# Part of a small triangular inverse moved from VectorE to GpSimd, in a two-layer hybrid decoder trunk

## Chip, core and metric

One core of a Trainium2 chip runs the whole kernel. The metric is device time in microseconds, the median of several runs.

## What is computed

A trunk of two layers over 528 positions (16 learned meta tokens and a sequence of 512) with a model width of 1024, all in float32. Each layer normalizes its input, projects it, and feeds four causal token mixers (RWKV-7, Mamba-2 SSD, retention, RG-LRU); the mixer outputs are projected, merged by gates and added to the stream, and a SwiGLU block follows. The change is in the RWKV-7 mixer, which the reference writes as a recurrence over positions:

```python
def step(s, inp):
    r_t, w_t, k_t, v_t, a_t, b_t = inp
    sa = jnp.einsum('bhvk,bhk->bhv', s, a_t)
    s = s * w_t[:, :, None, :] + sa[..., None] * b_t[:, :, None, :] + v_t[..., None] * k_t[:, :, None, :]
    return s, jnp.einsum('bhvk,bhk->bhv', s, r_t)
...
_, y = lax.scan(step, s0, xs)
```

with 16 heads of width 64. The kernel computes it in chunks of 64 positions. Within a chunk, the influence of each position on later ones is a strictly upper triangular matrix X, and the inverse of I - X is needed.

## The kernel before

Activations lie with 128 channels on the partitions and 528 positions in the free dimension. A dense product (`dense`, line 228) takes weight blocks of 128 x 128. `load_raw` fetches eight blocks in one load from SyncE, `blocks8` splits them into a high part (`whi`, ScalarE, line 217) and a low part (`wlo`, VectorE, line 218), and TensorE does three products for each block (line 240). `raw`, `whi` and `wlo` have three buffers each. Dense products fill most of TensorE's time in every stage.

The RWKV mixer goes through eight pairs of heads in each layer, so 16 times in all. For a pair, `rwkv_front` prepares the chunk operands, `rwkv_inverse` makes the triangular inverses, `rwkv_back` runs the nine chunks one after the other, and `rwkv_finish` normalizes. In `layer` (line 1103), the generator `others` gives the work of the other three mixers and of the gates, and `fill` puts a share of it behind each inverse and behind each back part. The order in which each engine runs its instructions is then fixed when the program is built, by priorities; each engine works through its own list in order.

`rwkv_inverse` does the following. TensorE makes the chunk matrices (line 867), VectorE masks them (lines 869 and 870). The 32 x 32 diagonal blocks are gathered through device memory: four stores into `xd` (line 905) and one load into `Xl` (line 909, tile `E`), so that each of 36 partitions (nine chunks times four blocks) holds a whole block. GpSimd sets `Nl` (tile `NS`) to the identity. Then 31 steps follow, a = 31 down to 1, of two VectorE instructions each: a multiplication (line 917, into `sm`) and an addition (line 919, into `NS`), on a rows by 32 - a columns. Each instruction needs the one before it. The result goes out to `nd` (line 920) and back in the layout of the chunks (lines 926 and 927). In `rwkv_back`, VectorE transposes blocks of it (line 941), and TensorE uses them first at line 951.

GpSimd otherwise clears pads and small blocks (lines 328, 709, 710, 771, 780, 885, 910, 911, 924 and others), copies (lines 784, 872, 963), and takes a share of the final scaling in `finish` (line 1237), where VectorE does the rest (line 1239).

Of the kernel before, what the change touches and what calls it, by code (L numbers as in the profile page):

```python
# [16 lines left out]
MUL, ADD, SUB, MIN, MAX = ALU.mult, ALU.add, ALU.subtract, ALU.min, ALU.max  # L17
# [4 lines left out]
T = 528  # L22
# [30 lines left out]
OTHERS = 8 * (2 * DENSE + 2.6) + DENSE + 4 * (6 * DENSE + 10.4) + 4 * (6 * DENSE + 14.3)  # L53
F1, F2, F3 = 48.0, 33.0, 170.0
UV = 2
GK = 2, 3, 3
NCST0, NCST1 = COFF["qdec"], COFF["hb"]

# [31 lines left out]
class _Em:  # L90
# [626 lines left out]
    def rwkv_common(self, l, S, p):  # L717
# [13 lines left out]
        def normed():  # L731
            self.X = [self.split(self.normed(j, S[j]), self.hp, "hh", "hl") for j in range(NT)]
            self.r = None
# [9 lines left out]
        for j in range(NT):  # L743
            if j == UV:
                normed()
# [105 lines left out]
    def rwkv_inverse(self, l, j, fr, p, q):  # L851
        nc = self.nc
        g2, AR, bk, P, v, bv = fr
        lo, hi = slice(0, 64), slice(64, 128)


        XK = self.t(q, [C64, 2, 64], "XK")
        MR = self.t(q, [C64, 2, 64], "MR")
        strict = self.c("tri")[:, :64].unsqueeze(1).unsqueeze(1)
        incl = self.c("tri")[:, 64:].unsqueeze(1).unsqueeze(1)  # L860
        blocks = [slice(b, b + 32) for b in range(0, 128, 32)]
        for c0 in range(0, C64, 2):
            n = min(2, C64 - c0)
            cs = slice(c0, c0 + n)
            ps = self.bank(self.psr).rearrange("p (c s x) -> p c s x", c=2, s=4)[:, :n]
            for c in range(c0, c0 + n):
                nc.tensor.matmul(ps[:, c - c0], bk[:, c].rearrange("p s x -> p (s x)"), AR[:, c],
                                 start=True, stop=True)
            nc.vector.tensor_tensor(out=XK[:, cs], in0=ps[:, :, 1:3], in1=strict.broadcast_to([128, n, 2, 64]), op=MUL)
            nc.vector.tensor_tensor(out=MR[:, cs], in0=ps[:, :, 0::3], in1=incl.broadcast_to([128, n, 2, 64]), op=MUL)  # L870
        for opp, h in ((hi, 0), (lo, 1)):
            nc.gpsimd.tensor_copy(AR[opp, :, 1 + h], XK[opp, :, h])


        BK = self.t(q, [C64, 2, 64], "BK")
        for c0 in range(0, C64, 4):
            n = min(4, C64 - c0)
            ps = self.bank(self.psr)[:, :n * 128]
            for c in range(c0, c0 + n):
                nc.tensor.transpose(ps[:, (c - c0) * 128:(c - c0 + 1) * 128], bk[:, c].rearrange("p s x -> p (s x)"),  # L880
                                    self.c("ident"))
            nc.scalar.activation(BK[:, c0:c0 + n].rearrange("p c h x -> p (c h x)"), ps, AF.Copy)

        SV = self.t(q, [C64, 2, 64], "SV")
        nc.gpsimd.memset(SV[lo, 0, 0], 0.0)
        nc.gpsimd.memset(SV[hi, 0, 1], 0.0)
        for c0 in range(0, C64, 8):
            n = min(8, C64 - c0)
            ps = self.bank(self.psr).rearrange("p (c x) -> p c x", c=8)
            for c in range(c0, c0 + n):  # L890
                for rows, opp in ((lo, hi), (hi, lo)):
                    nc.tensor.matmul(ps[opp, c - c0], v[rows, c * 64:c * 64 + 64], self.c("cent", rows)[:, rows],
                                     start=True, stop=True)
            nc.scalar.activation(SV[hi, c0:c0 + n, 0], ps[hi, :n], AF.Copy)
            nc.scalar.activation(SV[lo, c0:c0 + n, 1], ps[lo, :n], AF.Copy)


        i = self.ninv
        self.ninv += 1
        xd = self.tc.dram_tile([C64, 128, 32], F32, name=f"xd{i}")  # L900
        nd = self.tc.dram_tile([C64, 128, 32], F32, name=f"nd{i}")
        for h in range(2):
            for i in range(2):
                b = blocks[2 * h + i]
                nc.sync.dma_start(out=xd[:, b].rearrange("c r t -> r c t"), in_=XK[b, :, h, 32 * i:32 * i + 32])
        nl = 4 * C64
        Xl = self.t(q, 1056, "E", parts=nl)
        Nl = self.t(q, 2 * TP, "NS", parts=nl)
        nc.sync.dma_start(out=Xl[:, :1024], in_=xd.rearrange("c (g i) t -> (c g) (i t)", g=4))
        nc.gpsimd.memset(Nl[:, :1024], 0.0)  # L910
        nc.gpsimd.memset(Nl[:, :1024:33], 1.0)

        X3, N3 = (x[:, :1024].rearrange("p (i t) -> p i t", i=32) for x in (Xl, Nl))
        for a in range(31, 0, -1):
            w = 32 - a
            pr = self.t(q, 288, "sm", bufs=2, parts=nl)[:, :a * w].rearrange("p (i t) -> p i t", i=a)
            nc.vector.tensor_tensor(out=pr, in0=X3[:, :a, a:a + 1].broadcast_to([nl, a, w]),  # L917
                                    in1=N3[:, a:a + 1, a:].broadcast_to([nl, a, w]), op=MUL)
            nc.vector.tensor_tensor(out=N3[:, :a, a:], in0=N3[:, :a, a:], in1=pr, op=ADD)  # L919
        nc.sync.dma_start(out=nd.rearrange("c (g i) t -> (c g) (i t)", g=4), in_=Nl[:, :1024])  # L920
        N = self.t(q, 2 * TP, "NS").rearrange("p (c h x) -> p c h x", c=C64, h=2)
        for rows, h in ((lo, 0), (hi, 1)):
            b0, b1 = blocks[2 * h:2 * h + 2]
            nc.gpsimd.memset(N[rows, :, 1 - h], 0.0)
            nc.gpsimd.memset(N[b1, :, h, :32], 0.0)
            nc.sync.dma_start(out=N[b0, :, h, :32], in_=nd[:, b0].rearrange("c r t -> r c t"))
            nc.sync.dma_start(out=N[b1, :, h, 32:], in_=nd[:, b1].rearrange("c r t -> r c t"))
        return XK, MR, BK, SV, N

    def rwkv_back(self, l, j, fr, iv, p, q):  # L930
# [29 lines left out]

        UV = self.t(q, [C64, 2, 64], "XK")
        for rows, h in ((hi, 0), (lo, 1)):
            nc.gpsimd.tensor_copy(UV[rows, :, h], SV[rows, :, h])


        def flat(x):
            return x.rearrange("p h x -> p (h x)")

        for c in range(C64):
# [7 lines left out]
            with self.soon():  # L977
                for rows, h in heads:
                    nc.vector.tensor_copy(UV[rows, c, h], ps[rows, rows])
            if c == C64 - 1:  # L980
# [5 lines left out]
            ps = self.bank(self.psr)[:, :128]  # L986
            nc.tensor.matmul(ps, flat(BK[:, c]), flat(UV[:, c]), start=True, stop=True)
            with self.soon():
# [10 lines left out]
        for c0 in range(0, C64, 4):  # L999
            n = min(4, C64 - c0)  # L1000
            ps = self.bank(self.psr).rearrange("p (c h x) -> p c h x", c=4, h=2)
            for c in range(c0, c0 + n):
                o = ps[:, c - c0]
                fs = [lambda: nc.tensor.matmul(o, flat(UV[:, c]), MR[:, c], start=(c == 0), stop=True)]
                if c:
# [64 lines left out]
    def others(self, l, X, G, tg, tok, n, YB, YC, YD):  # L1070
# [3 lines left out]
        def gate(k):  # L1074
            for _ in range(k):
                b, m = next(gates, (None, None))
                if b is not None:
                    G[b][m] = self.gate(l, b, m, X, tg, tok, n)
                    yield DENSE

        def pool(name):
            self.st2.close()
            self.st2 = ExitStack()
            self.p2 = self.pool(name, 1, stack=self.st2)
# [3 lines left out]
        for j in range(8):  # L1088
            yield from self.lru(l, j, X, self.p2, YD)
            yield from gate(GK[0])  # L1090
        self.st2.close()
# [3 lines left out]
        for j in range(4):  # L1095
            yield from self.ret(l, j, X, self.p2, YC)
            yield from gate(GK[1])
        pool("ssm")
        for g in range(4):
            yield from self.ssm(l, g, X, self.p2, YB)  # L1100
            yield from gate(GK[2])

    def layer(self, l, S, sst, sd):
# [8 lines left out]
        with ExitStack() as st:  # L1112
# [9 lines left out]

            left, slots = OTHERS + DENSE * min(32, 8 * GK[0] + 4 * GK[1] + 4 * GK[2]), [w for _ in range(NT) for w in (F1, F2)]
            slots[-1] = F3
# [226 lines left out]
```

## Time and profile before

| | |
|---|---|
| median of 3 runs | 3492.44 us (3487.52 to 3496.19) |
| the profiled execution, its own time | 3490.24 us |
| its span, from the first to the last instruction | 3488.5 us |
| TensorE, VectorE, ScalarE, GpSimd busy | 96%, 69%, 44%, 5% of the span |

Engines are named PE (TensorE), PEld (its weight loads), DVE (VectorE), ACT (ScalarE), POOL (GpSimd) and SP (SyncE). Matmuls are pipelined, so PE's busy time overlaps itself; the distance between starts tells the pace. `Lnnn` is a line of the kernel, `out<-in` the tiles. A number in brackets behind an instruction is the engine's idle time before it, and who ended it. PEclk is the granted TensorE clock, 1.00 being 2.4 GHz and 0.50 being 1.2 GHz.

### The profile page before, as it was taken

The page shows a single profiled execution, that of the slowest core. Times are in us where ns is not written, and L with a number is a line of the kernel's source. Part 1 is how long each engine was busy: PE and PEld are TensorE (multiplying, and loading weights), DVE is VectorE, ACT ScalarE, POOL GpSimd, SP SyncE. Part 2 cuts the span into 40 slices and gives each one's busy share as a digit, 9 for nine tenths or more (in the row PEclk, how much of TensorE's full clock was granted, in tenths as well). Part 3 has the DMA queues.
Part 4 walks back from the last instruction along what each step waited for, and adds up shares of the span by engine and source line. Part 5 has one row for each costly group of instructions (what it writes and reads, how often), then busy time and mean ns, then how long its engine had stood idle before and what let it go on. Part 6 is the DMA issues. An engine that isn't in the chain of part 4 may idle for free. (4 is left out here: it accounts for less than half of the span.)

```text
span 3488.5 us, 61174 instructions
## 1 busy us (share of the span) xinstructions
PE 3363.5 (96%) x24584; PEld 3072.4 (88%) x24584; DVE 2396.4 (69%) x4644; ACT 1533.7 (44%) x2282; POOL 184.9 (5%) x493
## 2 busy tenths in 40 slices
PE   8999999999999999999999998999999989999998
PEld 7999899999988999999988887888888887788887
DVE  7877877788987555453348788678878885555543
ACT  6665544455444324222335654445454353332222
POOL 1000100100000000000000001010000000000001
PEclk9999999999999999999999998999999999999999
DMA  4333332233233643223333233223322245533332
GB/s 130 98 104 96 98 92 84 78 98 90 90 106 122 189 150 107 89 90 104 120 105 107 88 103 95 80 74 101 96 81 84 80 129 170 178 109 97 96 97 85
DMA packets 171739, 365.48 MB, mean 105 GB/s; under 512 B 54880, under 2 KB 63712, under 8 KB 171456
## 3 DMA queue, kind: packets, MB, share of 16 engines
q1 hardware_dynamic: 169936, 360.09, 33.6%
q8 instruction: 194, 3.18, 0.4%
q10 hardware_dynamic: 1152, 1.05, 0.1%
q14 instruction: 89, 0.73, 0.1%
q0 software_dynamic: 368, 0.44, 0.0%
HBM read 309.47 MB, written 47.71 MB: 102 GB/s over the span
## 5 line engine op out<-in xcount | busy, mean ns | idle before, releaser
L240 PE MATMUL d<-hh,whi 128*128 128x264 f32 (+1 forms) x4928 | 1181.6, 307 | 26.3 <-ACT whi L217 10.4
L240 PE MATMUL d<-hl,whi 128*128 128x264 f32 (+1 forms) x4928 | 1178.8, 306 | 1.2 <-DVE hl L259 1.1
L240 PE MATMUL d<-hh,wlo 128*128 128x264 f32 (+1 forms) x4928 | 1173.7, 305 | 0.0
L217 ACT ACTIVATE whi<-raw 128x1024 fp32r<-128x1024 f32 (+1 forms) x462 | 485.6, 1051 | 1158.7 <-PE d L240 920.0
L240 PEld LDWEIGHTS d<-hh,whi 128*128 128x128 f32 x4928 | 803.1, 190 | 64.2 <-ACT whi L217 10.4
L240 PEld LDWEIGHTS d<-hl,whi 128*128 128x128 f32 x4928 | 801.3, 190 | 34.6 <-DVE hl L259 2.4
L240 PEld LDWEIGHTS d<-hh,wlo 128*128 128x128 f32 x4928 | 800.5, 190 | 30.1 <-issue 1.2
L218 DVE TENSOR_TENSOR wlo<-raw,whi 128x1024 fp32r<-128x1024 f32 (+1 forms) x462 | 561.0, 1215 | 264.3 <-ACT whi L217 246.2
L240 PE MATMUL d<-yh,whi 128*128 128x264 f32 (+1 forms) x768 | 205.8, 324 | 2.4 <-ACT yh L258 2.4
L240 PE MATMUL d<-yl,whi 128*128 128x264 f32 (+1 forms) x768 | 207.4, 324 | 0.4 <-DVE yl L259 0.4
L240 PE MATMUL d<-yh,wlo 128*128 128x264 f32 (+1 forms) x768 | 206.4, 322 | 0.0
L917 DVE TENSOR_TENSOR sm<-E,NS 36x31 f32<-36x31 f32 (+15 forms) x496 | 164.0, 331 | 14.3 <-DMA E<-xd 4.7
L919 DVE TENSOR_TENSOR NS<-NS,sm 36x31 f32<-36x31 f32 (+15 forms) x496 | 164.2, 331 | 9.4
L240 PEld LDWEIGHTS d<-yh,whi 128*128 128x128 f32 x768 | 126.6, 188 | 16.6 <-ACT yh L258 5.4
L240 PEld LDWEIGHTS d<-yl,whi 128*128 128x128 f32 x768 | 127.8, 188 | 13.2 <-DVE yl L259 1.8
L240 PEld LDWEIGHTS d<-yh,wlo 128*128 128x128 f32 x768 | 127.5, 188 | 10.6
L240 PE MATMUL d<-fh,whi 128*128 128x264 f32 (+1 forms) x506 | 132.3, 318 | 0.0
L240 PE MATMUL d<-fl,whi 128*128 128x264 f32 (+1 forms) x506 | 132.0, 317 | 0.0
L240 PE MATMUL d<-fh,wlo 128*128 128x264 f32 (+1 forms) x506 | 131.6, 316 | 0.0
L1183 DVE TENSOR_TENSOR fg<-d,nr 128x528 f32<-128x528 f32 (+1 forms) x44 | 30.8, 700 | 126.0 <-PE d L240 122.4
L1066 DVE SCALAR_TENSOR_TENSOR gth<-gth,d 128x528 f32<-128x528 f32 (+1 forms) x48 | 33.4, 696 | 99.3 <-PE d L240 99.2
L1188 DVE TENSOR_TENSOR fth<-d,fth 128x528 f32<-128x528 f32 (+1 forms) x44 | 30.8, 700 | 92.6 <-PE d L240 92.5
(606 smaller groups left out, 4655.0 us busy)
## 6 DMA issues: line engine op xcount, KB each, us to landing
raw<-w SPq DMA_DIRECT2D x462, 512.0 KB
g<-gth SPq DMA_DIRECT2D x32, 264.0 KB
Bs<-acd SPq DMA_DIRECT2D x32, 264.0 KB
gth<-g SPq DMA_DIRECT2D x32, 264.0 KB
g<-gth SPq DMA_DIRECT2D x32, 256.0 KB
gth<-g SPq DMA_DIRECT2D x32, 256.0 KB
yd<-lt SPq DMA_DIRECT2D x16, 264.0 KB
ya<-wy SPq DMA_DIRECT2D x16, 264.0 KB
```

What stands on the lines that cost most here:

```text
L217: nc.scalar.activation(hi[:, :n], raw[:, :n], AF.Copy)
L218: nc.vector.tensor_tensor(out=lo[:, :n], in0=raw[:, :n], in1=hi[:, :n].bitcast(F32), op=SUB)
L240: nc.tensor.matmul(ps[:, h], w[:, k - k0], xv[:, h], start=(k == 0 and w is hi and xi == 0), stop=(k == nk - 1 and w is lo))
L917: nc.vector.tensor_tensor(out=pr, in0=X3[:, :a, a:a + 1].broadcast_to([nl, a, w]), in1=N3[:, a:a + 1, a:].broadcast_to([nl, a, w]), op=MUL)
L919: nc.vector.tensor_tensor(out=N3[:, :a, a:], in0=N3[:, :a, a:], in1=pr, op=ADD)
L1066: nc.vector.scalar_tensor_tensor(out=v2(th), in0=v2(th), scalar=1.0, in1=pz, op0=ADD, op1=MUL)
L1183: nc.vector.tensor_tensor(out=v2(g), in0=pg, in1=v2(r), op=MUL)
L1188: nc.vector.tensor_tensor(out=v2(th), in0=pu, in1=v2(th), op=MUL)
```

## The change

Column t of the inverse depends only on columns of the same index in rows below it, so the columns can be computed in two groups. The first 22 columns get a tile of their own, `Pl` (in the buffer `wy`), which GpSimd sets to the identity. GpSimd does 21 steps on it, a = 21 to 1, with the product in the buffer `wy2`, and copies the 22 x 22 result into `Nl` at the end. VectorE keeps columns 22 to 31 for all 31 steps. Both read the same loaded block `Xl`.

```diff
+PI = 22
...
+        Pl = self.t(p, T, "wy", parts=nl)[:, :PI * PI]
+        nc.gpsimd.memset(Pl, 0.0)
+        nc.gpsimd.memset(Pl[:, ::PI + 1], 1.0)
+        P3 = Pl.rearrange("p (i t) -> p i t", i=PI)
         for a in range(31, 0, -1):
-            w = 32 - a
+            t0 = max(a, PI)
+            w = 32 - t0
             pr = self.t(q, 288, "sm", bufs=2, parts=nl)[:, :a * w].rearrange("p (i t) -> p i t", i=a)
             nc.vector.tensor_tensor(out=pr, in0=X3[:, :a, a:a + 1].broadcast_to([nl, a, w]),
-                                    in1=N3[:, a:a + 1, a:].broadcast_to([nl, a, w]), op=MUL)
-            nc.vector.tensor_tensor(out=N3[:, :a, a:], in0=N3[:, :a, a:], in1=pr, op=ADD)
+                                    in1=N3[:, a:a + 1, t0:].broadcast_to([nl, a, w]), op=MUL)
+            nc.vector.tensor_tensor(out=N3[:, :a, t0:], in0=N3[:, :a, t0:], in1=pr, op=ADD)
+            if a < PI:
+                w = PI - a
+                pr = self.t(p, T, "wy2", parts=nl)[:, :a * w].rearrange("p (i t) -> p i t", i=a)
+                nc.gpsimd.tensor_tensor(out=pr, in0=X3[:, :a, a:a + 1].broadcast_to([nl, a, w]),
+                                        in1=P3[:, a:a + 1, a:].broadcast_to([nl, a, w]), op=MUL)
+                nc.gpsimd.tensor_tensor(out=P3[:, :a, a:], in0=P3[:, :a, a:], in1=pr, op=ADD)
+        nc.gpsimd.tensor_copy(N3[:, :PI, :PI], P3)
```

The lists of all engines come out in another order. GpSimd's list of the changed kernel, in the first inverse, holds the chain between the pad memset of a convolution (`xc`) and its next memsets. `wy` and its numbered forms are the tiles `Pl` and the product, `E` is the loaded block. Its line numbers are those of the changed kernel.

```order
L329 MEMSET xc 128x3 [waits DVE_49,PE_49,Pool_49]
L930 ISA
L930 TENSOR_TENSOR wy_786<-E,wy 36x21 [waits DMAHW0_49]
L932 TENSOR_TENSOR wy<-wy,wy_786 36x21 [waits Pool_49]
L930 TENSOR_TENSOR wy_792<-E,wy 36x40 [waits Pool_49]
L932 TENSOR_TENSOR wy<-wy,wy_792 36x20x2 [waits Pool_49]
```

The first multiplication waits for a DMA (the load of the block) alone, each later one for GpSimd's own instruction before it. The chain ends so:

```order
L932 TENSOR_TENSOR wy<-wy,wy_906 36x21
L933 COPY NS<-wy 36x22x22
L329 MEMSET xc 128x3
L781 MEMSET E 128x9
```

The next convolution's pad memset stands behind the chain and its copy.

VectorE's list around the end of the first inverse, before: the last addition (L919), then work on the next pair's `r` and its norms, then the transposes (L941).

```order
L778 SCALAR_TENSOR_TENSOR ech<-m_221,lam 128x576
L919 TENSOR_TENSOR NS<-NS,sm 36x31
L280 TENSOR_TENSOR r<-rtmp,v 128x528
L795 TENSOR_SCALAR rtmp<-s 128x264 x2
L218 TENSOR_TENSOR wlo<-raw,whi 128x1024
L713 SCALAR_TENSOR_TENSOR r<-d,par,r 128x528
L826 TENSOR_TENSOR AR<-r,E 64x9x64
L941 STREAM_TRANSPOSE sm<-NS 32x288
```

The same place in the changed kernel (L926 is the addition, L955 the transposes):

```order
L926 TENSOR_TENSOR NS<-NS,sm 36x10
L374 TENSOR_TENSOR th_1324<-th_1324,lt 128x528
L375 SCALAR_TENSOR_TENSOR lt<-la,th_1324 128x528
L376 TENSOR_TENSOR lt<-g_1314,lt 128x528
L219 TENSOR_TENSOR wlo<-raw,whi 128x1024
L714 SCALAR_TENSOR_TENSOR k<-d,par,k 128x528
L777 TENSOR_SCALAR lam<-lam 128x528
L779 SCALAR_TENSOR_TENSOR ech<-m_221,lam 128x576
L955 STREAM_TRANSPOSE sm<-NS 32x288 x2
```

The scan over `lam` (L778, now L779) stood ahead of the last addition and now stands behind it, and the work on `r` has gone behind the transposes: the inverse ends earlier in the list, measured by the other work around it.

## Rows read from the trace of the kernel before

**Rows 1.** The page: span, and busy time of each engine.

```profile
span 3488.5 us, 61174 instructions
...
PE 3363.5 (96%) x24584; PEld 3072.4 (88%) x24584; DVE 2396.4 (69%) x4644; ACT 1533.7 (44%) x2282; POOL 184.9 (5%) x493
```

**Rows 2.** Busy time by stage: per engine busy us and instructions, then granted clock, DMA share, GB/s.

```profile
60.00:1050.00 990.00, 964.27 (x8043) 910.53 (x8044) 797.25 (x1770) 512.69 (x808) 75.40 (x205) 0.99 0.31 95
...
1780.00:2860.00 1080.00, 1017.86 (x7589) 911.06 (x7590) 851.67 (x1861) 542.77 (x860) 80.00 (x219) 0.97 0.31 94
```

**Rows 3.** The same view of the 16 inverse windows: the first, the last, sum and mean.

```profile
78.70:119.70 41.00, 39.97 (x314) 39.05 (x312) 38.81 (x87) 31.69 (x42) 0.27 (x3) 1.00 0.36 106
...
2704.20:2750.40 46.20, 44.12 (x332) 41.27 (x331) 44.53 (x110) 14.96 (x21) 0.00 (x0) 1.00 0.36 110
sum 638.90, PE 623.20 PEld 592.04 DVE 591.97 ACT 371.77 POOL 12.68; mean PE 38.95 PEld 37.00 DVE 37.00 ACT 23.24 POOL 0.79
```

**Rows 4.** What PE waited for: us in total, times, longest.

```profile
PE s L951 <- DVE ends L556: 11.4, 1, 11.4
PE s L951 <- DVE sm L941: 11.0, 13, 2.6
```

**Rows 5.** Timeline of DVE and PE at the eleventh inverse, then the stretch after it.

```profile
2151.09 3.43 DVE L193 RECIPROCAL dtd<-dtd 16x528 f32<-16x528 f32 x1
...
2155.95 0.40 PE L240 MATMUL d<-hh,wlo 128*128 128x264 f32 x2
2167.77 0.31 PE L951 MATMUL s<-sm,XK 32*32 32x32 f32 x2 [11.42 <-DVE ends L556]
...
2167.50:2183.00 15.50, 12.37 (x120) 10.94 (x120) 10.04 (x27) 2.40 (x6) 2.39 (x4) 0.51 0.30 93
```

**Rows 6.** DVE groups by shape: busy us, mean ns, idle before.

```profile
L919 DVE TENSOR_TENSOR NS<-NS,sm 36x256 f32<-36x256 f32 x16 | 6.6, 411 | 0.2
...
L919 DVE TENSOR_TENSOR NS<-NS,sm 36x31 f32<-36x31 f32 x32 | 6.1, 191 | 0.4
```

**Rows 7.** DVE groups of lines 218 and 372.

```profile
L218 DVE TENSOR_TENSOR wlo<-raw,whi 128x1024 fp32r<-128x1024 f32 (+1 forms) x462 | 561.0, 1215 | 264.3 <-ACT whi L217 246.2 <-PE s L269 9.4 <-PE d L240 4.4
...
L372 DVE SCALAR_TENSOR_TENSOR th<-th,xc 128x528 f32<-128x528 f32 x16 | 11.2, 703 | 2.6 <-ACT th L354 2.4
```

**Rows 8.** Dense products on PE: start, us.

```profile
1200.15 0.41 PE L240 MATMUL d<-yh,whi 128*128 128x264 f32 x2
1200.39 0.40 PE L240 MATMUL d<-yl,whi 128*128 128x264 f32 x2
```

**Rows 9.** GpSimd lines 1237 and 784: ns min/median/max.

```profile
L1237 POOL TENSOR_TENSOR acc<-acc,fr x6: 724/909/966, 3474.1 to 3483.5; 128x256 f32<-128x256 f32 x6
...
L784 POOL COPY Pc<-E x16: 190/196/3197, 40.9 to 2616.7; 128x9 f32<-128x9 f32 x16
```

**Rows 10.** Two dependent GpSimd memsets: start, us.

```profile
2163.48 0.57 POOL L924 MEMSET NS<- 64x576 f32 x1 [1.02 <-DMA nd<-NS]
2164.11 0.33 POOL L925 MEMSET NS<- 32x288 f32 x1
```

**Rows 11.** Timeline at the end of the kernel, DVE and GpSimd.

```profile
3473.96 3.51 DVE L1239 SCALAR_TENSOR_TENSOR acc<-acc,par,fr 128x256 f32<-128x256 f32 x5
3477.91 0.42 DVE L1225 SCALAR_TENSOR_TENSOR acc<-d,acc 128x256 f32<-128x256 f32 x1 [0.43 <-PE d L250]
...
3474.08 2.72 POOL L1237 TENSOR_TENSOR acc<-acc,fr 128x256 f32<-128x256 f32 x3 [40.52 <-DVE fr L1233]
```

**Rows 12.** Timeline where GpSimd copies and DVE work meet.

```profile
1977.95 1.69 DVE L218 TENSOR_TENSOR wlo<-raw,whi 128x1024 fp32r<-128x1024 f32 x1
...
2159.27 3.20 POOL L784 COPY Pc<-E 128x9 f32<-128x9 f32 x1 [1.48 <-ACT E L782]
...
2161.00 0.74 DVE L821 TENSOR_TENSOR bk<-lam,ech 64x576 f32<-64x576 f32 x1
2161.67 0.74 DVE L822 TENSOR_TENSOR bk<-k,ech 64x576 f32<-64x576 f32 x1
```

## The prediction, made before the changed kernel ran

> **What bounds the kernel now.** I read the page's engine table first. TensorE (PE) is busy 96% of 3488.5 us, VectorE (DVE) 69%, GpSimd (POOL) 5% [rows 1]; less VectorE work alone therefore buys nothing. By stage, the first layer's mixers (60 to 1050 us) and the second's (1780 to 2860 us) leave PE 25.7 and 62.1 us idle [rows 2]. The inverses lie in these stages. So I next cut out the 16 stretches from the first L917 to the last L919 of each inverse, the "windows": 41.0 us the first, 46.2 us the last, 638.9 us in all. In them PE is busy 623.2 us and DVE 592.0 us, 37.0 of 39.9 us per window [rows 3]. Both engines are full there. DVE works in order, so the 62 small instructions of an inverse stand in one file with the weight splits (wlo, L218) that PE lives on. GpSimd is busy 0.8 us per window.
>
> What a late inverse costs can be seen too. PE also works in order, and L951, its first use of the inverse, stands among dense products. It waits there 22.4 us in 14 waits, one of 11.4 us, the others 2.6 us at most [rows 4]: the order puts L951 almost exactly where the inverse becomes ready, with no slack behind it. The one long wait is the price list. DVE lost 3.43 us to a reciprocal between two inverse instructions and more to its neighbours; PE finished its products at 2156.4 us and started L951 at 2167.8, doing nothing between. After it TensorE's granted clock was 0.51 for 15.5 us, the 1.2 GHz level of its two [rows 5], so some 7.6 us more went.
>
> **Part 1, what DVE loses.** The triangular sweep multiplies and adds a*(32-a) elements for a = 31 to 1, 5456 per operation kind. The corner of 22 columns is the sum of a*(22-a), 1771. The 62 instructions stay (a = 22 to 31 whole, the other 21 steps 10 columns wide); only elements go. A 36x256 addition takes 411 ns, a 36x31 one 191 [rows 6]: 0.98 ns per element. 2 x 1771 x 0.98 ns = 3.5 us per inverse. The order also takes other work out of the windows: 434 other DVE rows become 367, of which the wlo splits fall from 85 to 71. 14 x 1.22 us and 53 x 0.70 us [rows 7] over 16 make 3.4 us. So a window holds 6.9 us less DVE work.
>
> **Part 2, what PE loses in cover.** Counted in the order, the dense products between the last L867 and the first L951 of each inverse fall from 5321 to 4647 over the 16. Two take 0.24 us [rows 8]; 674 of them are 81 us, 5.1 us per inverse. PE arrives that much sooner. If nothing disturbed DVE, it would be ready 1.8 us before PE (6.9 - 5.1).
>
> **Part 3, what GpSimd adds.** 42 TENSOR_TENSORs in a chain, each waiting for the one before, 3542 elements, and a copy of 484. Before, L1237 is the only such instruction: 128x256, 724 ns at the fastest. The smallest copy, 128x9, takes 190 ns at the fastest [rows 9]. That gives about 0.19 us + 2.1 ns per element. Dependent GpSimd instructions stand 0.06 us apart (0.57 us long, 0.63 from start to start [rows 10]). Alone, the chain takes 42 x 0.25 + 3542 x 0.0021 = 17.9 us, the copy some 0.6 us. That fits in the 34.8 us (39.9 - 5.1) that a window would have; alone it would end before DVE's part. The two memsets of the new tile run earlier, while the block is still being loaded; GpSimd is idle there, so I cost them nothing (without that cover 0.6 us at most, as the larger memset of rows 10). The one ISA row ahead of the first multiplication stands before its wait too, in the first inverse only: nothing.
>
> **Part 4, the shared port.** The two parts do not run beside each other freely. At the end of the kernel, GpSimd's L1237 and DVE's L1239, each reading two SBUF tensors, meet: five DVE instructions take 3.51 us, where one alone of that size (L1225) takes 0.42 [rows 11]. Three GpSimd instructions thus cost DVE at least (3.51 - 2.10)/3 = 0.47 us each. Undisturbed DVE instructions overlap by 0.07 us (L821 and L822 start 0.67 us apart and take 0.74 [rows 12]), which makes it (3.51 - 1.82)/3 = 0.56; I take 0.52, 2.0 ns per element. In the mixers a wlo split took 1.69 us instead of 1.22 beside a GpSimd copy, and a 9-element copy 3.20 us instead of 0.19 behind DVE work [rows 7, 9, 12]. Each blocks the other. The inverse's DVE instructions have two SBUF inputs too. So the chain delays DVE: at least 0, if it fits into DVE's own pauses; at most its whole duration alone without the pauses, 42 x 0.19 + 7.4 + 0.6 = 16 us. By the finish's rate it is 3542 x 2.0 ns = 7.1 us, and I add 1 us of the fixed shares: **8 us**, since rows 11 show this pair of operations itself.
>
> **The sum.** Per inverse DVE is late by 8 - 1.8 = 6.2 us, and PE, in order and without slack, stands still as long. Slow clock after it: 7.6 us followed an 11.4 us wait; in proportion 4 us (bounds 0 and 7.6). 16 x 10.2 = 163 us. The 81 us of dense products taken out of the windows may fill PE's idle time elsewhere in the mixers, 25.7 + 62.1 - 15.7 = 72 us; most of it is short waits for results, so 12 us (bounds 0 and 72). 163 - 12 = +151. The profiled execution took 3490.24 us, 2.2 below the median of 3492.44; 3490 + 151 = 3641, and I say **3642 us** for the median. With 4 us of delay per inverse (stall 2.2, clock 1.5) it is 3537; with 12 (10.2 and 7) 3753.
>
> What queues behind: on GpSimd, the pad memsets of the next convolution and of E stand behind the chain; on SyncE, weight loads stand behind the store of the inverse. Both delays are the same microseconds, not others. The corner's tiles wy and wy2 belong to the back part's result, free before an inverse starts and wanted only after it: nothing.
>
> **Rivals.**
> - DVE waits for whole GpSimd instructions: the upper end above, 16 us of delay. Stall 16 - 1.8 = 14.2 us, clock 7.6: 16 x 21.8 - 12 = +337, 3827 us. For it: DVE's 1.69 us split beside a copy; against: at the finish a pair of instructions takes less than the 0.72 and 0.42 us of its two durations together [rows 9, 11]. The Trainium skill (SBUF — State Buffer, "Who interferes with whom") states it as a rule: the port pair that the two engines share is an exclusive lock, kept for the whole instruction, and a VectorE instruction with two SBUF inputs meets it when GpSimd reads. The trace agrees that they exclude each other; that the lock spans the whole duration it does not bear out.
> - GpSimd ends last. If each of its 42 instructions waits behind two DVE instructions rather than one (a window has 37.0 us for about 90, 0.41 us each), the chain takes 17.9 + 42 x 0.82 = 52 us, with the copy 18 us more than the 34.8. With 7.6 us of slow clock: 16 x 25.6 - 12 = +398, 3888 us. It decides from about one DVE instruction of wait each (35 us). For it: the 3.20 us copy; against: dependent DVE instructions leave a pause in which GpSimd gets in.
> - Faster: GpSimd's reads fall wholly into pauses (delay under 1.8 us per inverse). The waits at L951 (22.4 us) and the slow clock after the long one (7.6) go, and 12 us of filler: 3450 us. For it: 2.9 us of DVE idle per window; against: 7.1 us of reads, and rows 11.
> - No difference: a delay of 2 to 3 us, repaid by the filler; 3490 us.
> - That the change does not do what it says: the order shows the chain on GpSimd waiting for the load of the block alone, so the two sweeps may overlap. I give it nothing.
>
> **How the numbers follow.** Forecast 0.54, whole instructions 0.12, GpSimd last 0.16, faster 0.10, no difference 0.08. A measurement of this kernel tells 0.3%, about 10 us, from no change. Slower 0.82, the same 0.08, faster 0.10. The range leaves out the two cases that are not slower, 0.18: it runs from a little under 3537 to where GpSimd ends last, 3520 to 3890.
>
> **What would show it.** Right: the windows stay near 40 us though they hold less work; DVE's 36-partition steps lengthen by a few tenths where GpSimd overlaps; GpSimd's steps start 0.5 us or more apart; PE waits at the first use of the inverse some 6 us, 16 times, with 1.2 GHz stretches after. Wrong: windows of 33 to 35 us and no new waits of PE there (the ports do not matter), or the last GpSimd step well after DVE's (the second rival).

## The result and the profile after

| | before | changed |
|---|---|---|
| median of 4 runs, us | 3491.34 | 3520.53 |
| lowest to highest, us | 3487.52 to 3496.19 | 3518.92 to 3527.08 |
| profiled execution, us | 3490.24 | 3527.08 |
| its span, us | 3488.5 | 3525.3 |

The ratio is 1.0092, 95% interval 1.0078 to 1.0106: 29 us slower, where +151 was forecast. The sign was right, the size five times too large, and 3520.5 is the very lower end of the range.

The page of the changed kernel: span, then busy time of each engine (against [rows 1]).

```profile
span 3525.3 us, 61924 instructions
...
PE 3378.0 (96%) x24584; PEld 3082.0 (87%) x24584; DVE 2398.5 (68%) x4644; ACT 1535.6 (44%) x2282; POOL 558.5 (16%) x1213
```

Mean granted clock of TensorE, before:

```profile
core 0: 3488.5 us, clock 0.987
```

and of the changed kernel:

```profile
core 0: 3525.3 us, clock 0.983
```

Read PE first, since it is the busiest. The span grew by 36.8 us, some 7 more than the medians, as the profiled execution of the changed kernel is the slowest of its four. PE's work is the same 24584 matmuls, but its busy time grew by 14.5 us, and span less busy time from 125.0 to 147.3, by 22.3. Together they are the 36.8. The 14.5 us agree with the clock: (1 - 0.983) x 3525.3 - (1 - 0.987) x 3488.5 = 14.6, which can be 3.5 us off, as the clocks are rounded.

Then DVE. It was to lose 3.5 us per inverse, 56 us in all, yet its busy time is 2 us *higher* than before. The page's groups of instructions show where most of it came back:

```profile
L924 DVE TENSOR_TENSOR sm<-E,NS 36x60 f32<-36x60 f32 (+29 forms) x496 | 160.7, 324 | 16.2 <-DMA E<-xd 5.4
L926 DVE TENSOR_TENSOR NS<-NS,sm 36x60 f32<-36x60 f32 (+29 forms) x496 | 159.6, 322 | 10.8
...
L930 POOL TENSOR_TENSOR wy<-E,wy 36x21 f32<-36x21 f32 (+6 forms) x336 | 171.7, 511 | 89.7 <-DMA E<-xd 60.3
L932 POOL TENSOR_TENSOR wy<-wy,wy 36x21 f32<-36x21 f32 (+6 forms) x336 | 180.4, 537 | 26.1
```

DVE's multiplications and additions take 320.3 us, 20.0 per inverse; by their sizes (a line through the steps of before that ran undisturbed) they would take 16.9. On GpSimd one instruction takes 511 to 537 ns here.

The windows of the 16 inverses, first and last L924/L926, as in [rows 3] (stretch and length, then busy us and instructions of PE, PEld, DVE, ACT, POOL, then clock, DMA share, GB/s):

```profile
78.90:115.10 36.20, 32.28 (x240) 31.39 (x239) 34.05 (x81) 23.98 (x30) 22.16 (x45) 0.91 0.28 85
...
2725.60:2781.10 55.50, 50.52 (x377) 47.22 (x377) 48.35 (x120) 21.51 (x30) 23.81 (x43) 0.97 0.30 92
sum 579.10, PE 536.16 PEld 500.08 DVE 534.61 ACT 306.88 POOL 349.27; mean PE 33.51 PEld 31.25 DVE 33.41 ACT 19.18 POOL 21.83
```

A window has 36.2 us, 3.7 less than before, not the 40 of the forecast. What PE waited for, in us, times, longest:

```profile
PE s L270 <- issue: 18.1, 5, 4.1
PE s L965 <- DVE sm L955: 11.4, 9, 2.2
PE d L241 <- DVE x L334: 6.4, 3, 3.9
...
PE d L241 <- DVE NS L926: 5.5, 1, 5.5
```

L965 is the old L951, the first use of the inverse. PE waits there *less* than before, 11.4 us against 22.4 [rows 4], and in no wait longer than 2.2. The new waits are elsewhere: at dense products and at L270, the matmuls of a convolution, for DVE work that stands behind the sweep in DVE's file or in the middle of it. L270 is the old L269, where the kernel before had

```profile
PE s L269 <- issue: 2.3, 4, 0.7
```

("issue": the profile names nothing that the engine waited for). The timelines name it. In the first inverse, for example, the timeline (start, duration, engine, line) has on PE:

```profile
102.30 2.10 PE L270 MATMUL s<-xc,gw 128*128 128x264 f32 x4 [3.92 <-issue]
```

and on DVE the tile it wanted, xc, and the sweep's last step:

```profile
101.45 0.75 DVE L334 SCALAR_TENSOR_TENSOR xc<-d,par,xc 128x528 f32<-128x528 f32 x1
...
114.90 0.16 DVE L926 TENSOR_TENSOR NS<-NS,sm 36x10 f32<-36x10 f32 x1
```

xc ends at 102.2, and the matmul starts 0.1 us later. GpSimd's copy of the corner, the end of its chain, comes well before DVE's last step:

```profile
103.52 0.59 POOL L933 COPY NS<-wy 36x484 f32<-36x484 f32 x1
```

In all 16 inverses this copy ends ahead of DVE's last step, by 6.3 us at the least. So GpSimd does not end last; what it does is make DVE's steps longer.

### The profile page after: what moved, and what is told of

It reads as the page before. It is cut to its first block, busy times and chain, and to the rows that moved or that the text cites. A ratio compares the mean times of both kernels' runs of the same rounds, so it can differ in the third digit from the quotient of the medians.

```text
span 3525.3 us, 61924 instructions
## 1 busy us (share of the span) xinstructions
PE 3378.0 (96%) x24584; PEld 3082.0 (87%) x24584; DVE 2398.5 (68%) x4644; ACT 1535.6 (44%) x2282; POOL 558.5 (16%) x1213
## 5 line engine op out<-in xcount | busy, mean ns | idle before, releaser
L930 POOL TENSOR_TENSOR wy<-E,wy 36x21 f32<-36x21 f32 (+6 forms) x336 | 171.7, 511 | 89.7 <-DMA E<-xd 60.3
L932 POOL TENSOR_TENSOR wy<-wy,wy 36x21 f32<-36x21 f32 (+6 forms) x336 | 180.4, 537 | 26.1
L924 DVE TENSOR_TENSOR sm<-E,NS 36x60 f32<-36x60 f32 (+29 forms) x496 | 160.7, 324 | 16.2 <-DMA E<-xd 5.4
L926 DVE TENSOR_TENSOR NS<-NS,sm 36x60 f32<-36x60 f32 (+29 forms) x496 | 159.6, 322 | 10.8
```

Source lines behind the costliest of these rows:

```text
L926: nc.vector.tensor_tensor(out=N3[:, :a, t0:], in0=N3[:, :a, t0:], in1=pr, op=ADD)
L930: nc.gpsimd.tensor_tensor(out=pr, in0=X3[:, :a, a:a + 1].broadcast_to([nl, a, w]), in1=P3[:, a:a + 1, a:].broadcast_to([nl, a, w]), op=MUL)
L932: nc.gpsimd.tensor_tensor(out=P3[:, :a, a:], in0=P3[:, :a, a:], in1=pr, op=ADD)
```

## The experiments

The theory after the result: the shared port of Part 4 costs DVE 3.1 us per inverse, 49.6 of the 58 us that it should have lost and did not, and the kernel pays for it about one to one. Rivals: the order of instructions, which the change also rearranged, costs the time; GpSimd's mere length does; its pads, late behind the chain, do. Each kernel edits the changed one unless said otherwise, and each ratio is against the kernel before on the same chip.

### The same order, less reading by GpSimd: e1, e2, e3

In these three the orders of PE, DVE and SP are row for row those of the changed kernel (ACT's differs in one row's place in e1 and e2; GpSimd's own list differs). e1 leaves the corner out and puts two memsets per step, somewhat shorter, in the place of GpSimd's two instructions, so that GpSimd's chain writes and, apart from one copy of the block and one of the result, does not read:

```diff
-                nc.gpsimd.tensor_tensor(out=pr, in0=X3[:, :a, a:a + 1]...
-                nc.gpsimd.tensor_tensor(out=P3[:, :a, a:], ...
+                if a == PI - 1:
+                    nc.gpsimd.tensor_copy(pr[:, :a], Xl[:, :a])
+                m = min(100 + int(2.5 * a * w), 484)
+                nc.gpsimd.memset(pr[:, :m], 0.0)
+                nc.gpsimd.memset(Pl[:, :m], 0.0)
```

> Left out: GpSimd's products and sums of the corner. In their place stand one copy that waits for the block and then memsets, two per step, of about the same length (roughly 0.3 to 0.5 us each), which write SBUF and read nothing. The lists of TensorE, VectorE and SyncE are the same, row for row, as in the changed kernel. Theory 'port': the changed kernel is slower because GpSimd's reads hold up VectorE's instructions with two SBUF inputs (their time per inverse is 20.0 us, where their sizes alone would give 16.9); without the reads the 62 steps fall to about 17 us per inverse and the time falls by about 30 us, to 3490 or below. Theory 'queue': the pad memsets behind the chain make it slow; the time stays near 3520. Theory 'order': the new lists make it slow; the time stays near 3520 although the steps fall to 17 us.

Measured: 3471.43 us, ratio 0.9953 (0.9941 to 0.9965). Groups of instructions in e1:

```profile
L924 DVE TENSOR_TENSOR sm<-E,NS 36x60 f32<-36x60 f32 (+29 forms) x496 | 135.8, 274 | 15.5 <-DMA E<-xd 4.7
L926 DVE TENSOR_TENSOR NS<-NS,sm 36x60 f32<-36x60 f32 (+29 forms) x496 | 134.9, 272 | 10.8
...
L934 POOL MEMSET wy<- 36x152 f32 (+6 forms) x336 | 119.6, 356 | 18.7
L933 POOL MEMSET wy<- 36x152 f32 (+6 forms) x336 | 118.1, 352 | 19.0
```

The steps take 270.7 us, 16.9 per inverse: as by size. DVE's busy time over the whole kernel is 2348.6 us, 49.9 below the changed kernel's, of which these two lines give 49.6. So all that GpSimd's reads cost DVE lies in these two lines: 3.1 us per inverse, 74 ns for each of 672 GpSimd instructions. Windows of e1, same view as above:

```profile
sum 530.10, PE 523.61 PEld 492.53 DVE 483.65 ACT 307.52 POOL 112.22; mean PE 32.73 PEld 30.78 DVE 30.23 ACT 19.22 POOL 7.01
```

33.1 us each, 3.1 less. GpSimd is busy 7.0 us per window here against 21.8: half of the memsets do not wait for the block, and many run ahead of the sweep. 287 of the 672 lie inside it, beside 240 of DVE's 992 steps, and those 240 take on average some 3 ns more than the others, by size. In the first, the convolution's wait of 3.92 us is one of 0.20:

```profile
101.08 1.13 PE L270 MATMUL s<-xc,gw 128*128 128x264 f32 x4 [0.20 <-issue]
```

e2 has the same edit with `m = min(8, 484)`, short memsets.

> As the run with the memset chain, but each memset covers 8 columns (about 0.1 us), so the chain takes some 5 to 8 us instead of 18 to 25; same lists again. Port: the same time as with the longer memset chain, within 4 us. Queue: clearly faster than it, by most of the 30 us. Order: both stay near 3520.

Measured: 3469.77 us, 0.9952 (0.9938 to 0.9966), steps 16.9. The length of the memsets makes no difference. But in both kernels GpSimd's chain also ends sooner than in the changed one (in the first inverse of e1 at 90.3 us, not 103.5), so a late end of the chain is tested by e3 and e4 and not here.

e3 keeps GpSimd's instructions but lets them do half the rows:

```diff
-                nc.gpsimd.tensor_tensor(out=pr, in0=X3[:, :a, a:a + 1]...
+                nc.gpsimd.tensor_tensor(out=pr[:, :(a + 1) // 2], in0=X3[:, :(a + 1) // 2, a:a + 1]...
...
-                nc.gpsimd.tensor_tensor(out=P3[:, :a, a:], ...
+                nc.gpsimd.tensor_tensor(out=P3[:, :(a + 1) // 2, a:], ...
```

> Left out: about half of the corner's rows in each GpSimd step; the 42 products and sums work on half of the elements, the lists of TensorE, VectorE, ScalarE and SyncE are those of the changed kernel. Port: VectorE's 62 steps take about 18.5 us per inverse, halfway between 16.9 and 20.0, and the time lies about halfway between the changed kernel and the memset chain, 3500 to 3510. Order or queue: 3515 to 3520.

Measured: 3484.65 us, 0.9993 (0.9985 to 1.0001), a miss below the 3500 to 3510 expected; the steps:

```profile
L924 DVE TENSOR_TENSOR sm<-E,NS 36x60 f32<-36x60 f32 (+29 forms) x496 | 143.0, 288 | 16.1 <-DMA E<-xd 5.3
L926 DVE TENSOR_TENSOR NS<-NS,sm 36x60 f32<-36x60 f32 (+29 forms) x496 | 142.9, 288 | 10.8
```

They take 17.9 per inverse: half the reads cost a third of the delay, not half. The timelines say why. In the changed kernel, at the same steps of the first inverse, GpSimd:

```profile
83.61 0.39 POOL L930 TENSOR_TENSOR wy<-E,wy 36x105 f32<-36x105 f32 x1
84.07 0.40 POOL L932 TENSOR_TENSOR wy<-wy,wy 36x105 f32<-36x105 f32 x1
84.55 0.40 POOL L930 TENSOR_TENSOR wy<-E,wy 36x112 f32<-36x112 f32 x1
85.03 0.41 POOL L932 TENSOR_TENSOR wy<-wy,wy 36x112 f32<-36x112 f32 x1
```

and DVE beside it:

```profile
84.22 0.46 DVE L924 TENSOR_TENSOR sm<-E,NS 36x192 f32<-36x192 f32 x1
84.72 0.45 DVE L926 TENSOR_TENSOR NS<-NS,sm 36x192 f32<-36x192 f32 x1
85.19 0.47 DVE L924 TENSOR_TENSOR sm<-E,NS 36x207 f32<-36x207 f32 x1
```

Before, without GpSimd, the same two steps on DVE:

```profile
82.92 0.35 DVE L917 TENSOR_TENSOR sm<-E,NS 36x192 f32<-36x192 f32 x1
83.31 0.35 DVE L919 TENSOR_TENSOR NS<-NS,sm 36x192 f32<-36x192 f32 x1
```

In e3, DVE:

```profile
84.05 0.35 DVE L924 TENSOR_TENSOR sm<-E,NS 36x192 f32<-36x192 f32 x1
84.44 0.35 DVE L926 TENSOR_TENSOR NS<-NS,sm 36x192 f32<-36x192 f32 x1
```

and GpSimd:

```profile
84.27 0.29 POOL L930 TENSOR_TENSOR wy<-E,wy 36x56 f32<-36x56 f32 x1
...
84.64 0.31 POOL L932 TENSOR_TENSOR wy<-wy,wy 36x56 f32<-36x56 f32 x1
```

Alone, DVE's steps start 0.39 us apart. Beside GpSimd steps 0.48 apart, DVE's stand 0.47 to 0.50 apart. Beside GpSimd steps 0.37 apart, they keep their 0.39. And 0.46 to 0.49 is GpSimd's own pitch at this size, as the last inverse of the changed kernel shows in a stretch with no DVE instruction beside it:

```profile
2742.11 0.38 POOL L930 TENSOR_TENSOR wy<-E,wy 36x112 f32<-36x112 f32 x1
2742.57 0.42 POOL L932 TENSOR_TENSOR wy<-wy,wy 36x112 f32<-36x112 f32 x1
2743.06 0.37 POOL L930 TENSOR_TENSOR wy<-E,wy 36x105 f32<-36x105 f32 x1
```

The two chains go **in lockstep**, at the pitch of the slower. My reading of it, argued and not shown, is that each reads while the other stands between two of its dependent instructions. Only what GpSimd's pitch exceeds DVE's own is lost, not the whole of its reads. It holds beyond this pair: over the 320 DVE steps of the changed kernel that are followed directly by the next and have a GpSimd step beside them, the mean pitch is 428 ns, and the mean of the longer of the two own pitches (each a line by size through undisturbed steps) is 431; in e3, over 298 steps, it is 361 against 365.

Time follows the steps: 16.9, 17.9, 20.0 us per inverse give 3471, 3485, 3520.5. From the first to the last, 16 x 3.1 = 49.6 us of steps make 49.1 us of time (48.5 by the two ratios). In this one order GpSimd's reads are thus the cause of nearly all of it, with at most some 6 us left for the pads (e4); the rest of the change, without them, gains 17 us. It also settles Part 1's size: a window of e1 holds 30.2 us of DVE work against 37.0 before [rows 3], 6.8 less.

### The pads behind the chain: e4

In the changed kernel DVE waited 5.4 + 1.1 us for L329, the pads of the next convolution, which stand behind the chain on GpSimd (tile and line that waited, us, times):

```profile
  DVE x L334: 5.4, 2
  DVE Bs L334: 1.1, 1
```

```diff
-        nc.gpsimd.memset(xc[:, T:T + 3], 0.0)
+        nc.vector.memset(xc[:, T:T + 3], 0.0)
```

> The pad memsets of the convolutions (48 of them, 0.1 us each on GpSimd) go to VectorE; all else as in the changed kernel, so no convolution waits behind the GpSimd chain. The lists change in some places. Queue: the time falls by 15 us or more. Port or order: within 8 us of the changed kernel, since only 6.5 us of VectorE's waits in the changed kernel are for these memsets.

Measured: 3515.45 us, 1.0083 (1.0070 to 1.0095), steps 20.1. The 5 us fit the 6.5 of the trace, but the intervals overlap: at most a small part.

### Smaller corners: e5, e6

```diff
-PI = 22
+PI = 16
```

> The corner is 16 columns instead of 22: 30 GpSimd instructions of at most 64 elements. All lists change. Theory 'lockstep': two chains of dependent instructions pass the port to and fro, so a VectorE step is stretched only to GpSimd's own pitch (0.25 us + 2.1 ns per element, 0.28 to 0.385 us here) where that is longer than its own (0.24 to 0.45 us). Summed over the 30 overlapped steps that is about 0.6 us per inverse: the 62 steps take 19.7 us, where their sizes alone give 19.1. Theory 'sum of holds' (2.0 ns for each GpSimd element is added to VectorE, as at the end of the kernel): 1360 elements x 2.0 ns = 2.7 us, 21.8 us. The time by lockstep is 3475 to 3490, no slower than before; by the sum 3500 or more.

Measured: 3481.64 us, 0.9980 (0.9970 to 0.9990); steps 19.9, where size alone makes 19.1, the expected lockstep 19.7 and the sum of GpSimd's reads 21.8 (1360 elements x 2.0 ns more). With `PI = 18`:

> The corner is 18 columns: 34 GpSimd instructions of at most 81 elements (pitch up to 0.42 us). Lockstep: the 62 steps take about 1.2 us more than the 18.5 us of their sizes alone, 19.7; time 3480 to 3495. Sum of holds: 1938 elements x 2.0 ns = 3.9 us more, 22.4 us; time 3505 or more.

Measured: 3499.16 us, 1.0032 (1.0020 to 1.0045); steps 19.9 (alone 18.5, lockstep 19.7, sum of reads 22.4). The steps speak for lockstep both times. The time of e6 lies above what its steps explain, and e5 and e6 have the same 19.9 yet stand 17.5 us apart. Their orders differ from each other and from the changed kernel's; that is the only other difference I know of, and e11 returns to it.

### One operand out of SBUF: e7

If the port is the cause, a DVE step that reads only one tensor from SBUF should not be stretched. The product goes to PSUM, so that the addition reads one operand from each; the multiplication still reads two from SBUF:

```diff
-            pr = self.t(q, 288, "sm", bufs=2, parts=nl)[:, :a * w].rearrange("p (i t) -> p i t", i=a)
+            pr = self.bank(self.psr)[:nl, :a * w].rearrange("p (i t) -> p i t", i=a)
```

> As the changed kernel with 22 columns, but VectorE's product goes to a PSUM bank instead of SBUF, so its additions have one SBUF input only. Port: the additions are no longer stretched; the wait stays with the products. The sum of the 62 steps' excess falls from 3.1 us to about half or less (apart from what PSUM itself adds, the same for each addition), GpSimd's chain gets shorter than 25.4 us, and the time lies under 3510. If the inputs do not matter (a plain rivalry of the two engines for SBUF): the additions stay as long as the products, time near 3520.

Measured: 3480.02 us, 0.9975 (0.9967 to 0.9984). Groups in e7:

```profile
L924 DVE TENSOR_TENSOR s<-E,NS 36x60 f32<-36x60 f32 (+29 forms) x496 | 163.8, 330 | 18.5 <-DMA E<-xd 7.6 <-ACT SV L896 0.6
L926 DVE TENSOR_TENSOR NS<-NS,s 36x60 f32<-36x60 f32 (+29 forms) x496 | 132.7, 268 | 10.7 <-DVE s L924 0.2
```

The addition takes 268 ns, as undisturbed in e1 (272); the multiplication still 330. Half of the delay is gone. That is shown by the steps; the time has an order of its own in it. A miss: GpSimd's chain did not get shorter, 25.3 us from its first to its last step against 25.4.

### The chain without the relief: e8

DVE does all 32 columns again (`t0 = a`), GpSimd computes its corner as well, and the copy of the result, which nobody uses, is left out.

> VectorE does all 32 columns as in the kernel before; GpSimd does its 42 instructions too, and its result is not used. This shows the price of the chain alone. Lockstep: the 62 steps take about 3 us more than 20.5, some 23.5 us per inverse, and the time is 40 to 55 us over the kernel before. Sum of holds: 27 us per inverse and 100 us or more. Only the lists matter: 20.5 us and no difference in the steps.

Measured: 3518.02 us, 1.0089 (1.0075 to 1.0103):

```profile
L924 DVE TENSOR_TENSOR sm<-E,NS 36x31 f32<-36x31 f32 (+15 forms) x496 | 188.1, 379 | 11.1 <-DMA E<-xd 1.1
L926 DVE TENSOR_TENSOR NS<-NS,sm 36x31 f32<-36x31 f32 (+15 forms) x496 | 185.5, 374 | 9.6
```

23.3 us per inverse against 20.5 by size: 2.8 us of delay, near the 3.1 of the changed kernel and far from the 27 us per inverse of the sum of holds. The time grew by 30 us, less than the 45 of the delay: a miss in the time. Its order is its own too.

### Both together: e9, e10

The product in PSUM, with PI = 16:

> Both remedies together: a corner of 16 columns, and VectorE's product in PSUM. Lockstep and port: the steps' excess over their sizes falls from 0.8 us (corner of 16 alone) to about 0.5 us per inverse, some 19.6 us; if the 0.8 us were the whole remaining price, the time is 3470 to 3482. If the gain of either came from its lists and not from the port, the two do not add and the time lies anywhere between 3475 and 3500.

Measured: 3480.88 us, 0.9984 (0.9976 to 0.9993), steps 19.7. Against e5 that is 0.2 us less in the steps and no difference in time. With PI = 18:

> A corner of 18 columns with the product in PSUM. Port: the excess falls from 1.4 us (corner of 18 alone) to about 0.8 us, the steps to 19.3 us per inverse, and the time falls below the 3499 of the corner of 18 by 10 us or more. Lists: it may fall or rise by up to 15 us whatever the steps do.

Measured: 3468.71 us, **0.9945** (0.9931 to 0.9959), steps 19.3:

```profile
L924 DVE TENSOR_TENSOR s<-E,NS 36x112 f32<-36x112 f32 (+29 forms) x496 | 163.4, 329 | 17.6 <-DMA E<-xd 8.0
L926 DVE TENSOR_TENSOR NS<-NS,s 36x112 f32<-36x112 f32 (+29 forms) x496 | 145.8, 294 | 10.1
```

It beats both kernels. The excess over the size, 0.8 us, is as expected; that steps of 19.3 us give a shorter time than the 19.7 of e9, 12 us, is more than 16 x 0.4.

### What an order alone does: e11, e12

e11 is the kernel *before* with e7's edit, no GpSimd part at all. It takes no work from DVE and adds none.

> The kernel before, without any GpSimd chain, with VectorE's product in PSUM. Port: nothing contends, so there is nothing to win; the 62 steps stay at about 20.5 us per inverse (21 if PSUM is a little slower to reach) and the time stays within 8 us of the kernel before. If the product in PSUM is a gain by itself, the time falls by 8 us or more.

Measured: 3518.44 us, 1.0092 (1.0076 to 1.0109): a plain miss. The steps are unchanged:

```profile
L917 DVE TENSOR_TENSOR s<-E,NS 36x31 f32<-36x31 f32 (+15 forms) x496 | 167.8, 338 | 13.8 <-DMA E<-xd 3.3 <-ACT SV L895 1.3 <-DVE R L486 0.2
L919 DVE TENSOR_TENSOR NS<-NS,s 36x31 f32<-36x31 f32 (+15 forms) x496 | 161.7, 326 | 9.1
...
PE s L951 <- DVE sm L941: 26.2, 13, 14.7
```

20.6 us per inverse, but 32 us more time. The edit changed the order in which the kernel's instructions stand. It also makes the sweep take turns with the mixer's matmuls in the two PSUM banks of `psr`; of that the trace shows at most 1.5 us (DVE's waits for L895 and L486, above), so I put the time down to the order, which is argued and not shown. The wait of 14.7 us at L951 is not new: it is the 11.4 us of [rows 4], grown by 3.3. As there, the reciprocal stands between two steps of the eleventh sweep:

```profile
2161.83 3.43 DVE L193 RECIPROCAL dtd<-dtd 16x528 f32<-16x528 f32 x1
```

So a kernel whose steps are as long as before can differ by as much as the whole result, and of all these runs only e1 to e3, with the changed kernel's own order, isolate the port.

e12 drops the corner from both engines (DVE's half of the sweep stays), with an order of its own:

> Left out: the corner altogether (no tile, no GpSimd chain, no copy); VectorE keeps its 62 narrower steps. The lists are new ones again, different from those of the changed kernel and of the kernel before. If the 17 us that the memset chain gained come from the shorter steps, the time is again 3465 to 3475. If they came from that one set of lists, the time lies anywhere between 3465 and 3515, since the product in PSUM moved the kernel before by 32 us with steps of unchanged length. Steps in either case: 16.9 us per inverse.

Measured: 3467.19 us, 0.9938 (0.9926 to 0.9951), steps 16.9. Shorter steps and a new order are together worth 17 us in e1 and 21 here. The expectation gave the order alone 3465 to 3515, so this run does not tell the two apart.

## Why the prediction was right in sign and wrong in size

- **What bounds the kernel**: right. PE waits in order for DVE's work near the inverses; with the order held, 49 us of DVE steps were 49 us of time. Between the two profiled spans of e1 and the changed kernel, 3469.7 and 3525.3 us, PE's busy time grew by 18.4 us (3359.6 to 3378.0, at a granted clock of 0.988 and 0.983) and its idle time by 37.2.
- **Part 1**, 3.5 us less in the steps and 6.9 less per window: measured 3.6 (20.5 to 16.9) and 6.8.
- **Part 2**, 5.1 us less cover: the products between L867 and L951 are 5321 before and 4647 after in the traces too, as counted. The 1.8 us that DVE would be ready ahead of PE no run shows: in e1 PE's busy time per window fell by 6.2 us, but PE is nearly full in both, so this only follows the window, 6.8 us shorter.
- **Part 3**, GpSimd chain of 17.9 us alone: 25.4 in the kernel (21.3 to 28.6 over the 16), beside DVE, and it ended before DVE's part. The rival in which GpSimd ends last fell with this; it began at 35 us and put the chain at 52.
- **Part 4 is the step that failed.** "By the finish's rate it is 3542 x 2.0 ns = 7.1 us, and I add 1 us of the fixed shares: 8 us": measured 3.1. The finish [rows 11] was the right pair of operations but the wrong situation. There five DVE instructions queue up and want the port without a pause, so every GpSimd read may cost its length; that they do not wait for one another is read from the code, and this was not tried apart. In the sweep each DVE step waits for the one before, and by my reading GpSimd reads in that pause. The price measured is the difference of two pitches, not a sum of reads. The prediction itself wrote "at least 0, if it fits into DVE's own pauses" and chose the other end.
- **The sum** with 3.1 in it: DVE late by 3.1 - 1.8 = 1.3 us, clock in the forecast's proportion 0.8, 16 x 2.1 - 12 = +22, 3512 us. The rest, some 8 us, may be the pads or a spare time smaller than the 1.8 us, which no run measured; that is open. The sum would put a kernel level with the one before at 2.3 us of delay; e3 is level at 1.0.
- **The place of the waits** was wrong: not 6 us at the first use of the inverse, 16 times, but at convolutions (18.1 us at L270, 2.3 before) and products in the middle of the sweep. I had followed only the sweep's result. Everything that stands behind a longer sweep in DVE's file is late as well, and those tiles had PE waiting before the inverse did.
- **"Both delays are the same microseconds"**, of the pads: up to 6.5 us by the trace, some 5 by e4, not separable from none.
- **Whole instructions** as rival: not borne out. 16 us of delay would have been needed. Were whole instructions kept apart, GpSimd's 0.40 us and DVE's undisturbed 0.35 would make a pitch of 0.75 in the timelines above; it was 0.48. The Trainium skill (SBUF — State Buffer, "Who interferes with whom") also says which instructions meet at the port at all: VectorE's with two SBUF inputs, and only against a GpSimd instruction that reads SBUF. There the runs agree with it: memsets cost nothing (e1), and an addition with one operand in PSUM was not stretched (e7, 268 ns).
- **The faster rival** asked for a delay under 1.8 us per inverse. e1, with none, is that case in the changed kernel's order, at 3471.4 us, and e10, with 0.8, stands at 3468.7, where the rival said 3450. So the sum also overrates what the change brings without the port, by some 21 us.
- **No difference** asked for a delay of 2 to 3 us, repaid by the filler. The delay came close to it with 3.1, and was not repaid.

What stays open: how much of the 17 us that e1 gains is the relief and how much its order, and how much of e5 to e10 is order. No kernel with before's order and a shorter sweep was run. One place of the order may be all of it. The kernel before lost 11.4 us and up to 7.6 of slow clock where a reciprocal stands inside the eleventh sweep [rows 5]. In the changed kernel and in every run but e11 that reciprocal stands outside; in e1 the sweep ends at 2128.7 us, the reciprocal starts at 2178.2, and no wait at the first use of the inverse (L967) is longer than 2.1 us:

```profile
L194 DVE RECIPROCAL dtd<-dtd x2: 3430/3436/3441, 414.2 to 2178.2; 16x528 f32<-16x528 f32 x2
...
PE s L967 <- DVE sm L957: 11.7, 11, 2.1
```

e8 fits this: it has no relief at all, and is 15 us faster than its longer steps would make it.

## What to carry to other kernels

Price two engines that share a port by what they do between instructions: in this case two chains of dependent steps lost what the slower pitch exceeded the faster, while the queued instructions at the end of the kernel lost about the whole of the other's reads [rows 11]. Before giving part of a chain to GpSimd, compare its step with VectorE's and keep the part small enough that its pitch is not longer. One operand of VectorE's steps in PSUM takes that step out of GpSimd's way (e7), but whether it saves time has to be measured in each kernel (e9: nothing; e11: 32 us lost). Where an edit reorders a whole program, undo the suspected cost with the order held fixed (e1 to e3) before believing any difference of one per cent.

## What the runs showed of the hardware

- A chain of dependent GpSimd steps that read SBUF and one of DVE steps with two SBUF operands go at the pitch of the slower: DVE's 36x192 step starts every 0.39 us alone, 0.47 to 0.50 beside GpSimd steps 0.48 apart (0.46 to 0.49 alone), 0.39 beside steps 0.37 apart.
- GpSimd memsets of 352 to 356 ns on average, beside 240 of DVE's 992 steps in e1, did not lengthen them (272 to 274 ns on average over all, the size's own time).
- Reading one operand from PSUM cost DVE's addition no more than from SBUF at these sizes (326 ns in e11 against 331 in the kernel before, no GpSimd beside it), and took the step out of GpSimd's way (268 ns in e7).
